# Down product of the last stage: all 1024 output columns at once in two passes over Strassen products, instead of two halves of 512 columns

## The chip, the cores and the metric

The kernel runs on one core of one Trainium2 chip. The metric is the device time of one execution in microseconds; where several runs are given, their median.

## The reference

The reference is one encoder layer on 512 tokens of width 1024 in float32. The part that changes is the last matrix product and the norm behind it:

```
h2 = rmsnorm(x1, g_pre_ffn)                       # x1: (512, 1024)
hid = depthwise_conv3(h2 @ w_up) + conv_b         # (512, 5632)
a, b = split(hid, 2)
y = x1 + rmsnorm((gelu(a) * b) @ w_down, g_post_ffn)   # w_down: (2816, 1024)
```

## The kernel before, in words

Every float32 matrix is held as a high part (rounded to the 32-bit format that TensorE multiplies at full pace) and a low part, and every product is three matmuls: high by high, high by low, low by high. A weight is prepared in one chain. SyncE loads a block of 128 rows by 1024 columns (512 KB) from `wall` into one of four `raw` buffers. ScalarE copies it to its high part (L100), VectorE subtracts that to get the low part (L119, function `split`). The parts lie in nine `w4` slots. `w_get` hands out the next unit of the list `units`, and prepares as many units ahead as slots allow; which instruction stands where on each engine is then set by a scheduler that orders the whole program ahead of time, each engine executing its own list in order.

The down product multiplies the gated hidden values `gp` (2816 features, 512 tokens) by `w_down`. Of its 22 blocks of 128 features, 18 are taken as nine couples (`DP`, index j), on which one level of Strassen's scheme (the Winograd form) runs: the two feature blocks of a couple, two halves of the tokens and two halves of the columns are its 2x2 matrices. That makes 7 products M1 to M7 in place of 8. The token side of the sums (A11, S1 to S4 and so on, function `down_forms`, names `fh`, `fl`, `fa`) is computed earlier on VectorE. The last four blocks (`WHOLE`) are multiplied without Strassen (`add_whole`, L1388).

Before, the columns are done in two halves of 512, each half a full sweep over the nine couples. A couple has two weight units. A "q" unit holds the three plain quarters (768 columns, loaded from memory), a "t" unit four sums (1024 columns) that VectorE forms by an add on 512 columns (L226) and two on 256 (L230, L231). Each of the 7 products fills one PSUM bank with two tiles of 128 tokens by 256 columns, so a couple is 42 matmuls with 256 columns (L1372). The eighth bank (M8) takes whole blocks. Behind the first half VectorE combines the banks into c11 to c22 (L1401 to L1417); behind the second, `token` adds the whole blocks, combines, scales (L1470 to L1488) and `rows` multiplies by the norm, adds x1 (L1520) and writes out. The norm's power is one GpSimd instruction on one column (L1488, `qr`). In the names of the profile, `dh` and `dl` are the high and low parts of a down unit, `wh` and `wl` those of a whole block, `cv` are convolution steps of the stage ahead, whose last part runs beside the start of the down product.

## Time and profile before

| | us |
|---|---|
| median of 3 runs (783.43 to 784.63) | 783.65 |
| span of the profiled execution | 782.6 |
| the down product: its first matmul starts, its last matmul starts | 668.8, 775.4 |
| busy TensorE / VectorE / ScalarE / GpSimd | 774.5 / 639.5 / 485.2 / 103.5 |

The span is that of one execution under the profiler, and all rows of the trace belong to it. In rows of instructions, the first number is the start and the second the duration, in microseconds; since an engine overlaps the end of one instruction with the next, the distance between starts is what an instruction costs. An "x" gives a count. A row of waits gives the microseconds waited in total, how often, and the longest.

### The profile page before, as it was taken

The page shows a single profiled execution, that of the slowest core. Times are in us where ns is not written, and L with a number is a line of the kernel's source. Part 1 is how long each engine was busy: PE and PEld are TensorE (multiplying, and loading weights), DVE is VectorE, ACT ScalarE, POOL GpSimd, SP SyncE. Part 2 cuts the span into 40 slices and gives each one's busy share as a digit, 9 for nine tenths or more (in the row PEclk, how much of TensorE's full clock was granted, in tenths as well). Part 3 has the DMA queues.
Part 4 walks back from the last instruction along what each step waited for, and adds up shares of the span by engine and source line. Part 5 has one row for each costly group of instructions (what it writes and reads, how often), then busy time and mean ns, then how long its engine had stood idle before and what let it go on. Part 6 is the DMA issues. An engine that isn't in the chain of part 4 may idle for free.

```text
span 782.6 us, 13472 instructions
## 1 busy us (share of the span) xinstructions
PE 774.5 (99%) x5139; PEld 720.7 (92%) x5139; DVE 639.5 (82%) x1093; ACT 485.2 (62%) x878; POOL 103.5 (13%) x132
## 2 busy tenths in 40 slices
PE   9999999999999999999999999999999999999996
PEld 8888998998999999999998998999999998999996
DVE  6567987789789988877765679989999889886987
ACT  7555568688466766644454686657777568644542
POOL 0040001130021102033211200001111012200001
PEclk9999999999999999999999999999999999999998
DMA  8783224453223233233459120435555375733344
GB/s 288 271 246 102 81 82 162 108 122 108 81 91 126 82 122 121 83 110 106 138 171 337 54 81 28 124 107 141 142 148 149 108 199 111 171 114 107 109 162 162
DMA packets 35889, 104.80 MB, mean 134 GB/s; under 512 B 4400, under 2 KB 6320, under 8 KB 35824
## 3 DMA queue, kind: packets, MB, share of 16 engines
q1 hardware_dynamic: 27936, 87.81, 34.0%
q0 software_dynamic: 7024, 14.95, 9.0%
q10 hardware_dynamic: 864, 1.18, 0.4%
q8 instruction: 40, 0.66, 0.4%
q14 instruction: 25, 0.20, 0.1%
HBM read 91.34 MB, written 4.19 MB: 122 GB/s over the span
## 4 chain that ended last, share of the span: by engine, by line
PE 92%; DVE 3%; DMA 3%; issue 1%; ACT 0%; POOLq 0%; DVEq 0%; POOL 0%; ACTq 0%
PE ps L926 24%; PE ps L300 12%; PE ps L302 12%; PE ps L301 12%; PE ps L1372 7%; PE ps L755 5%; PE ps L634 4%; PE ps L636 4%; PE ps L635 4%; DMA raw<-wall 3%; PE ps L1109 2%; PE ps L1108 2%; PE ps L1107 2%; DVE dl L119 1%; PE ps L997 1%
## 5 line engine op out<-in xcount | busy, mean ns | idle before, releaser
L119 DVE TENSOR_TENSOR wl<-raw,wh 128x1024 fp32r<-128x1024 f32 (+1 forms) x84 | 96.0, 1152 | 54.3 <-issue 19.1
L100 ACT ACTIVATE wf<-raw 128x512 fp32r<-128x512 f32 x140 | 85.6, 625 | 67.3 <-PE ps L301 19.4
L926 PE MATMUL ps<-sh,wf 128*128 128x256 f32 x640 | 117.4, 276 | 0.1
L119 DVE TENSOR_TENSOR wf<-raw,wf 128x512 fp32r<-128x512 f32 x140 | 107.0, 774 | 9.2 <-ACT wf L100 8.6
L926 PEld LDWEIGHTS ps<-sh,wf 128*128 128x128 f32 x640 | 101.9, 192 | 1.1 <-ACT sig L100 0.5
L100 ACT ACTIVATE wh<-raw 128x1024 fp32r<-128x1024 f32 (+2 forms) x88 | 84.8, 977 | 28.5 <-DMA raw<-wall 14.0
L300 PE MATMUL ps<-h2h,wh 128*128 128x512 f32 (+1 forms) x256 | 90.6, 354 | 0.0
L301 PE MATMUL ps<-h2l,wh 128*128 128x512 f32 (+1 forms) x256 | 90.4, 353 | 0.0
L302 PE MATMUL ps<-h2h,wl 128*128 128x512 f32 (+1 forms) x256 | 90.4, 353 | 0.0
L926 PE MATMUL ps<-sl,wf 128*128 128x256 f32 x320 | 88.0, 275 | 0.0
L926 PEld LDWEIGHTS ps<-sl,wf 128*128 128x128 f32 x320 | 61.4, 192 | 0.4
L1372 PE MATMUL ps<-dh,fh 128*128 128x256 f32 x216 | 59.6, 276 | 0.3 <-DVE yy L1409 0.3
L1372 PE MATMUL ps<-dl,fh 128*128 128x256 f32 x216 | 59.5, 275 | 0.0
L1372 PE MATMUL ps<-dh,fl 128*128 128x256 f32 x216 | 59.4, 275 | 0.0
L100 ACT ACTIVATE dh<-raw 128x768 fp32r<-128x768 f32 (+1 forms) x36 | 33.6, 950 | 33.8 <-DVE raw L231 15.2
L302 PEld LDWEIGHTS ps<-h2h,wl 128*128 128x128 f32 x256 | 48.6, 190 | 5.1
L301 PEld LDWEIGHTS ps<-h2l,wh 128*128 128x128 f32 x256 | 48.6, 190 | 4.5
L300 PEld LDWEIGHTS ps<-h2h,wh 128*128 128x128 f32 x256 | 48.6, 190 | 4.5
L926 PE MATMUL ps<-xh,wf 128*128 128x256 f32 x288 | 52.2, 275 | 0.0
L636 PE MATMUL ps<-wh,xl 128*128 128x512 f32 x128 | 48.5, 379 | 0.0
L635 PE MATMUL ps<-wl,xh 128*128 128x512 f32 x128 | 48.5, 379 | 0.0
L634 PE MATMUL ps<-wh,xh 128*128 128x512 f32 x128 | 48.5, 380 | 0.0
(343 smaller groups left out, 2171.6 us busy)
## 6 DMA issues: line engine op xcount, KB each, us to landing
raw<-wall SPq DMA_DIRECT2D x144, 512.0 KB, 3.7
x<-x SPq DMA_DIRECT2D x24, 256.0 KB, 6.0
fl<-gp POOLq DMA_DIRECT2D x12, 256.0 KB, 3.8
swap<-qkraw POOLq DMA_DIRECT2D x16, 128.0 KB, 4.8
x<-x POOLq DMA_DIRECT2D x8, 256.0 KB, 2.3
fl<-fs POOLq DMA_DIRECT2D x8, 256.0 KB, 4.3
xT<-xT SPq DMA_DIRECT2D x7, 256.0 KB, 5.0
xT<-xT POOLq DMA_DIRECT2D x4, 256.0 KB, 4.1
```

The source lines that it names most:

```text
L100: return nc.scalar.activation(out=o, in_=i, func=AF.Copy)
L119: low[0] = nc.vector.tensor_sub(lo, src, as32(hi)).ins
L300: nc.tensor.matmul(o, ah, bh, start=start, stop=False, skip_group_check=skip)
L301: nc.tensor.matmul(o, ah, bl, start=False, stop=False, skip_group_check=skip)
L302: pe_last[0] = nc.tensor.matmul(o, al, bh, start=False, stop=stop, skip_group_check=skip).ins
L634: nc.tensor.matmul(acc[t], xh[k][:, c], turns(wh[:, f]), start=k == 0, stop=False)
L635: nc.tensor.matmul(acc[t], xh[k][:, c], turns(wl[:, f]), start=False, stop=False)
L636: part_end[0] = nc.tensor.matmul(acc[t], xl[k][:, c], turns(wh[:, f]), start=False, stop=k == KD - 1)
L755: nc.tensor.matmul(bank[t], a_[:, c], turns(w_[:, f]), start=first and k == i == 0, stop=last and k == 3 and i == 2, skip_group_check=True,)
L926: self.last = nc.tensor.matmul(o, w_[:, c], a_, start=first and k == n == 0, stop=k == 3 and n == 2, skip_group_check=True,)
L1107: nc.tensor.matmul(o, ah, turns(bh), start=k == 0, stop=False)
L1372: nc.tensor.matmul(o, a_[:, c], turns(w_[:, f]), start=j == t == i == 0, stop=j == DP - 1 and i == 2 and n not in (M2, M3, M4), skip_group ...
```

## The change

All 1024 columns are done at once, so the two halves of the columns in Strassen's scheme are now the two halves of 512 of the whole width, and each product fills two PSUM banks (one tile of 128 tokens by 512 columns each). Eight banks hold four products, so the nine couples are swept twice. Pass 1 makes M1, M6, M5 and M4 (weights: the units "da" and "db", two products from each), pass 2 makes M2, M3 and M7 (units "dc" and "dd"). Matmuls have 512 columns, 24 per couple in pass 1 and 18 in pass 2; the last token tile's last part is still done in two halves of 256.

Each unit "da", "db", "dc" is one load of 512 KB, "dd" one of 256 KB. In "da" VectorE adds the loaded halves (L234); in "db" VectorE adds one piece (L236) and GpSimd another (L237), then `split` (now L121) follows; in "dd" VectorE adds one piece (L225). All whole blocks are used in pass 2's end, and two of them also in pass 1, after the couples 3 and 5 (`FILL`), so these two are loaded twice. The combination of the banks is L1408 (M6), L1412 (M5) and L1416 (M4) between the passes and L1468, L1470, L1478, L1484, L1488, L1497 at the end; the last step of the norm is L1447, its power L1440.

The core of the diff:

```diff
-            for _ in range(2):
-                pairs = [[("q", i + j), ("t", i + j)] for j in range(DP)]
-                whole = [[("blk", i + DP)], [("blk", i + DP + 1)]]
-                for u in pairs[:4] + whole[:1] + pairs[4:6] + whole[1:] + pairs[6:] if i == DOWN0 else pairs + whole:
-                    units += u
-                i += DP + WHOLE // 2
+            for j in range(DP):
+                units += [("da", j), ("db", j)] + ([("blk", WHOLE0 + FILL.index(j))] if j in FILL else [])
+            for j in range(DP):
+                units += [("dc", j), ("dd", j)]
+            units += [("blk", WHOLE0 + n) for n in range(WHOLE)]
+            i = NW
...
-    def w_down(form, i):
-
-        if form == "q":
-            raw = w_raw["q"] = raw_tile()
-            nc.sync.dma_start(raw, wall[i])
-            raw = raw[:, : 3 * 256]
+    def w_down(form, j):
+
+        i = DOWN0 + 2 * j
+        if form == "dd":
+            raw = raw_tile()[:, :S]
+            nc.sync.dma_start(raw, wall[i, :, S:])
+            nc.vector.tensor_add(raw, raw, w_raw["b"][:, S:])
+            w = slot("dt", 0, 1088)
+            lo, hi = w[:, AT_64 : AT_64 + S], w[:, S + AT_192 : 2 * S + AT_192]
         else:
-            b, raw = w_raw["q"], raw_tile()
-            two = "p (n c) -> p n c"
-            nc.vector.tensor_tensor(
-                out=raw[:, :512].rearrange(two, n=2), in0=b[:, :512].rearrange(two, n=2),
-                in1=b[:, None, 768:].to_broadcast([P, 2, 256]), op=ALU.add,
-            )
-            nc.vector.tensor_add(raw[:, 512:768], raw[:, :256], b[:, 256:512])
-            nc.vector.tensor_add(raw[:, 768:], raw[:, 512:768], b[:, 512:768])
-        w = 768 if form == "q" else 1024
-        at = 0 if form == "q" and (i - DOWN0) % (DP + WHOLE // 2) < 2 else AT_192
-        hi, lo = slot("dh", at, w), slot("dl", at, w)
+            raw = raw_tile()
+            nc.sync.dma_start(raw, wall[i + (form != "da")])
+            b1, b2 = raw[:, :S], raw[:, S:]
+            if form == "da":
+                w_raw["a"] = b2
+                nc.vector.tensor_add(b2, b1, b2)
+            elif form == "db":
+                nc.vector.tensor_add(b2, w_raw["a"], b2)
+                nc.gpsimd.tensor_tensor(out=b1, in0=b2, in1=b1, op=ALU.add)
+            else:
+                w_raw["b"] = raw
+            hi, lo = slot("dh", AT_192), slot("dl", AT_192)
...
+    def two_banks():
+        return [ps(), ps()]
+
+    def product(bank, w, at, act, j, first=0, last=DP - 1):
+
+        ah, al = dforms[j][act]
+        f = slice(at * S, (at + 1) * S)
+        for t in range(2):
+            c = slice(t * P, (t + 1) * P)
+            for i, (a_, n) in enumerate(((ah, 0), (ah, 1), (al, 0))):
+                nc.tensor.matmul(
+                    bank[t], a_[:, c], turns(w[n][:, f]), start=j == first and i == 0, stop=j == last and i == 2,
+                    skip_group_check=True,
+                )
...
+    m1, m6, m5, m4 = (two_banks() for _ in range(4))
     late = list(range(EAGER, DP))
-    c11, c12, c21, c22 = c4 = hi192("c", F32), lo64("c", F32), blk(n="c"), blk(n="c")
-    e1, e3, uu, yy = tmp("e1"), tmp("e3"), tmp("uu"), tmp("yy")
-
-    def after6():
-        v.tensor_add(uu, m[M6], e1)
-        v.tensor_sub(c12, m[M5], uu)
-        v.tensor_add(c12, c12, e3)
-
-    freed = []
-
-    def after7():
-        v.tensor_add(e1, m[M7], uu)
-        freed.append(v.tensor_sub(yy, m[M5], e1).ins)
-        v.tensor_add(c22, c22, yy)
-
-    steps = {
-        M1: lambda: copy(e1, m[M1]),
-        M2: lambda: v.tensor_add(c11, m[M2], e1),
-        M3: lambda: copy(e3, m[M3]),
-        M6: after6, M7: after7,
-        M4: lambda: v.tensor_add(c21, m[M4], e1),
-    }
+    ee = [hi192("c", F32), lo64("c", F32)]
+    pq, qq, uu = halves("c"), halves("c"), [tmp("uu") for _ in range(2)]
     for j in range(DP):
+        end = j == DP - 1
         if j < WHOLE:
             whole.append(two_parts(gp[2 * DP + j]))
         if j == 4:
             down_forms(late.pop(0))
-        products(m, j, *((steps, LOOK - 1) if j == DP - 1 else ()))
-        if j in (3, 5):
+        wa = w_get()
+        product(m1, wa, 0, "A11", j)
+        if end:
+            for t in range(2):
+                copy(ee[t], m1[t])
+        wb = w_get()
+        product(m6, wb, 1, "S2", j)
+        if end:
+            for t in range(2):
+                v.tensor_add(uu[t], m6[t], ee[t])
+        product(m5, wa, 1, "S1", j)
+        if end:
+            for t in range(2):
+                v.tensor_sub(pq[t], m5[t], uu[t])
+        product(m4, wb, 0, "A22", j)
+        if end:
+            for t in range(2):
+                v.tensor_add(qq[t], m4[t], uu[t])
+        if j in FILL:
             w = w_get()
-            for t in range(NT):
-                add_whole(m, t, [j // 2 - 1], [w], j == 5)
-            if j == 5:
-                copy(c22, m[M8])
+            for t in range(2):
+                add_whole(m4[t], 2 + t, [FILL.index(j)], [w])
...
+    m2, m3, m7 = (two_banks() for _ in range(3))
+    yy = halves("e")
     for j in range(DP):
+        wc = w_get()
+        if j < DP - 1:
+            product(m2, wc, 0, "A12", j, last=None)
+            product(m3, wc, 1, "S4", j, last=None)
+            product(m7, w_get(), 0, "S3", j)
         if j == 0:
             gpf.extend((hi192("gpf", F32), lo64("gpf", F32)))
             for i in range(2):
                 nc.gpsimd.dma_start(gpf[i], gffn[None, i * S : (i + 1) * S].to_broadcast([P, S]))
+    for t in (2, 0, 1, 3):
+        xt[t] = halves("x1")
+        for n in range(2):
+            nc.sync.dma_start(xt[t][n], x1[t][n])
+    product(m7, w_get(), 0, "S3", j)
+    for t in range(2):
+        v.tensor_add(qq[t], m7[t], qq[t])
+        square(2 + t, 0, qq[t])
+        v.tensor_sub(yy[t], pq[t], m7[t])
+    product(m2, wc, 0, "A12", j, last=None)
+    product(m3, wc, 1, "S4", j, last=None)
+    m8 = two_banks()
+    ww = [w_get() for _ in range(WHOLE)]
+    for t in range(2):
+        weighted(2 + t, 0, qq[t])
+    add_whole(m8[0], 2, (0, 1), ww[2:], None, True, True)
+    v.tensor_add(yy[0], m8[0], yy[0])
+    square(2, 1, yy[0])
+    weighted(2, 1, yy[0])
+    waiting = 2, scale(2, qn[2][:, 0:1], qn[2][:, 1:2])
+    for t in range(2):
+        add_whole(m2[t], t, (0, 1), ww[:2], None, False, True)
+        v.tensor_add(ee[t], m2[t], ee[t])
+        square(t, 0, ee[t])
+        weighted(t, 0, ee[t])
+        add_whole(m3[t], t, (0, 1), ww[2:], None, False, True)
+        v.tensor_add(pq[t], m3[t], pq[t])
+        square(t, 1, pq[t])
+        rows(*waiting)
+        waiting = t, scale(t, qn[t][:, 0:1], qn[t][:, 1:2])
+        weighted(t, 1, pq[t])
+    t = NT - 1
+    parts_ = (T0, slice(0, P)), (T1, slice(P, 256))
+    for n, (f, half) in enumerate(parts_):
+        add_whole(m8[1][:, f], t, (0, 1), ww[2:], half, n == 0, n == 1)
+        v.tensor_add(yy[1][:, f], m8[1][:, f], yy[1][:, f])
+        square(t, 1 + n, yy[1][:, f])
+        if n == 0:
+            v.scalar_tensor_tensor(
+                out=qn[t][:, 3:4], in0=qn[t][:, 0:1], scalar=EPS, in1=qn[t][:, 1:2], op0=ALU.add, op1=ALU.add
+            )
+            rows(*waiting)
+            weighted(t, 1, yy[1], f)
+    sc = scale(t, qn[t][:, 3:4], qn[t][:, 2:3], 0.0)
+    weighted(t, 1, yy[1], T1)
+    rows(t, sc, ((0, 512), (512, 768), (768, 1024)))
```

Order on VectorE around the fourth and fifth couple of pass 1 (numbers behind a name are buffers' numbers; `raw_7575` and `raw_7588` are the fourth couple's "da" and "db", 7618 the first whole block, 7630 and 7659 the fifth couple). Before, in the first half of the columns, at the fourth couple:

```order
L119 TENSOR_TENSOR dl_7619<-raw_7614,dh_7618 128x1024
L226 TENSOR_TENSOR raw_7708<-raw_7674 128x512
L119 TENSOR_TENSOR wl_7653<-raw_7650,wh_7652 128x1024
L230 TENSOR_TENSOR raw_7708<-raw_7708,raw_7674 128x256
L1291 TENSOR_TENSOR gp_7054<-gp_7054 128x256
L231 TENSOR_TENSOR raw_7708<-raw_7708,raw_7674 128x256
L1292 TENSOR_TENSOR gp_7054<-gp_7065,fs_7823 128x256
L119 TENSOR_TENSOR fl_7829<-fs_7823,fh_7828 128x512
L119 TENSOR_TENSOR dl_7677<-raw_7674,dh_7676 128x768
```

After:

```order
L121 TENSOR_TENSOR dl_7579<-raw_7575,dh_7578 128x1024
L121 TENSOR_TENSOR dl_7593<-raw_7588,dh_7592 128x1024
L234 TENSOR_TENSOR raw_7630<-raw_7630 128x512
L1297 TENSOR_TENSOR gp_7054<-gp_7054 128x256
L121 TENSOR_TENSOR fl_7727<-fs_7721,fh_7726 128x512
L1298 TENSOR_TENSOR gp_7054<-gp_7065,fs_7721 128x256
L121 TENSOR_TENSOR fl_7731<-gp_7065,fh_7730 128x512
L236 TENSOR_TENSOR raw_7659<-raw_7630,raw_7659 128x512
L121 TENSOR_TENSOR wl_7621<-raw_7618,wh_7620 128x1024
L234 TENSOR_TENSOR raw_7673<-raw_7673 128x512
L121 TENSOR_TENSOR dl_7634<-raw_7630,dh_7633 128x1024
L121 TENSOR_TENSOR fl_7735<-gp_7054,fh_7734 128x512
```

The three adds that form a "t" unit are gone; each unit now has one 512-column add ahead of a 1024-column subtract, two such units per couple, and an add stands up to six places ahead of the subtract of its own unit.

Order on GpSimd around the end of the convolution; the DMAs form the low parts of activations. Before:

```order
L1273 DMA fl_7398<-fs_7392 128x512
L1273 DMA fl_7403<-gp_6622 128x512
L1273 DMA fl_7408<-gp_6611 128x512
L1273 DMA fl_7496<-fs_7490 128x512
L1273 DMA fl_7501<-gp_6855 128x512
L1273 DMA fl_7506<-gp_6844 128x512
L1540 DMA gpf_8248<-gffn 128x512
```

After:

```order
L1279 DMA fl_7399<-fs_7393 128x512
L237 TENSOR_TENSOR raw_7445<-raw_7445 128x512
L1279 DMA fl_7404<-gp_6622 128x512
L1279 DMA fl_7409<-gp_6611 128x512
L237 TENSOR_TENSOR raw_7545<-raw_7545 128x512
L1279 DMA fl_7498<-fs_7492 128x512
L1279 DMA fl_7503<-gp_6855 128x512
L1279 DMA fl_7508<-gp_6844 128x512
L237 TENSOR_TENSOR raw_7588<-raw_7588 128x512
```

GpSimd has an add of 128x512 per couple of pass 1 between those DMAs and behind them.

Order on VectorE at the change of passes: 7834 and 7847 are the last couple of pass 1, 7873 with 7885, 7909 with 7915 and 7929 with 7971 the first three couples of pass 2 ("dc" with "dd"). Before, at the change of column halves (L1414 to L1417 combine the banks):

```order
L119 TENSOR_TENSOR dl_8092<-raw_8087,dh_8091 128x1024
L1414 TENSOR_TENSOR c_7511<-ps_7536,e_1282_7515 128x512
L119 TENSOR_TENSOR dl_8143<-raw_8140,dh_8142 128x768
L1401 TENSOR_TENSOR uu_7517<-ps_7565,e_1282_7515 128x512
L1402 TENSOR_TENSOR c_7512<-ps_7558,uu_7517 128x512
L1408 TENSOR_TENSOR e_1282_7515<-ps_7572,uu_7517 128x512
L1403 TENSOR_TENSOR c_7512<-c_7512,e_1283_7516 128x512
L1409 TENSOR_TENSOR yy_7518<-ps_7558,e_1282_7515 128x512
L119 TENSOR_TENSOR dl_8190<-raw_8185,dh_8189 128x1024
L1410 TENSOR_TENSOR c_7514<-c_7514,yy_7518 128x512
```

After:

```order
L225 TENSOR_TENSOR raw_7885<-raw_7885,raw_7873 128x512
L121 TENSOR_TENSOR dl_7838<-raw_7834,dh_7837 128x1024
L121 TENSOR_TENSOR dl_7852<-raw_7847,dh_7851 128x1024
L121 TENSOR_TENSOR dl_7876<-raw_7873,dh_7875 128x1024
L121 TENSOR_TENSOR dt_7888<-raw_7885,dt_7888 128x512
L225 TENSOR_TENSOR raw_7915<-raw_7915,raw_7909 128x512
L121 TENSOR_TENSOR dl_7912<-raw_7909,dh_7911 128x1024
L1408 TENSOR_TENSOR uu_7526<-ps_7514,c_7520 128x512
L1408 TENSOR_TENSOR uu_7527<-ps_7515,c_7521 128x512
L1412 TENSOR_TENSOR c_7522<-ps_7516,uu_7526 128x512
L225 TENSOR_TENSOR raw_7971<-raw_7971,raw_7929 128x512
L121 TENSOR_TENSOR dt_7918<-raw_7915,dt_7918 128x512
```

The adds that read the banks M6 and M5 (L1408, L1412) now stand behind the second L225, and the third L225 between them; before, a subtract or two stood there and no add on a loaded block.

Order on VectorE at the very end. Before:

```order
L1470 TENSOR_TENSOR z_8895<-ps_8772,e_8184 128x256
L1480 SCALAR_TENSOR_TENSOR q_8180<-q_8180 128x1
L1520 SCALAR_TENSOR_TENSOR zg_8436<-zg_8436,qr_8850,x_1463_8820 128x512
L1487 TENSOR_TENSOR qs_8898<-q_8180 128x1
L1520 SCALAR_TENSOR_TENSOR zs_8849<-zs_8849,qr_8850,x_1464_8821 128x512
L1477 TENSOR_TENSOR zs_8896<-z_8895,gpf_8249 128x256
L1520 SCALAR_TENSOR_TENSOR zg_8564<-zg_8564,qr_8897,x_1471_8867 128x512
L1520 SCALAR_TENSOR_TENSOR zs_8896<-zs_8896,qr_8897,x_1472_8868 128x256 x2
```

After:

```order
L1435 TENSOR_TENSOR zs_8394<-e_7970,gpf_8002 128x256
L1447 SCALAR_TENSOR_TENSOR zs_8347<-zs_8347,qr_8368,x_1429_8223 128x512
L1500 SCALAR_TENSOR_TENSOR q_7962<-q_7962 128x1
L1447 SCALAR_TENSOR_TENSOR zs_8372<-zs_8372,qr_8368,x_1430_8224 128x512
L1497 TENSOR_TENSOR e_7970<-ps_8264,e_7970 128x256
L1435 TENSOR_TENSOR zs_8394<-e_7970,gpf_8002 128x256
L1439 SCALAR_TENSOR_TENSOR qs_8412<-q_7962 128x1
L1447 SCALAR_TENSOR_TENSOR zs_8267<-zs_8267,qr_8411,x_1431_8227 128x512
L1447 SCALAR_TENSOR_TENSOR zs_8394<-zs_8394,qr_8411,x_1432_8228 128x256 x2
```

Of the two last-but-one steps of the third written tile (L1520 before, L1447 after, each 128x512), both stood behind the last add from PSUM (L1470); now they stand ahead of it (L1497).

167 lines of the change are left out of this document (35 added, 132 removed).

## Prediction

> **What bounds the kernel now.** I read the page's totals first, then the chain of waits, then the waits of TensorE in the last stage.
>
> ```profile
> span 782.6 us, 13472 instructions
> PE 774.5 (99%) x5139; PEld 720.7 (92%) x5139; DVE 639.5 (82%) x1093; ACT 485.2 (62%) x878; POOL 103.5 (13%) x132
> PE 92%; DVE 3%; DMA 3%; issue 1%; ACT 0%; POOLq 0%; DVEq 0%; POOL 0%; ACTq 0%
> 668.92 15.98 PE ps L1372 x143
> PE ps L1372 <- DVE yy L1409: 0.3, 1, 0.3
> ```
>
> TensorE is busy for 99% of the span and is 92% of the chain. In the stage that changes it waits once, 0.3 us, at the change of column halves. So the stage is worth what its matmuls take, as long as the weight work of VectorE stays ahead; whatever makes a weight late is added in full. The profiled execution spans 782.6 us, 1.05 below the median of 783.65; I add that 1.05 at the end.
>
> **Matmuls: 4.4 us less.** The timeline of TensorE gives the two paces and the ends of the stage (the first row of each pair is 16 matmuls ahead of the second).
>
> ```profile
> 662.50 0.38 PE L301 MATMUL ps<-h2l,wh 128*128 128x512 f32 x1
> ...
> 665.95 0.38 PE L302 MATMUL ps<-h2h,wl 128*128 128x512 f32 x1
> ...
> 668.76 0.27 PE L1372 MATMUL ps<-dh,fa 128*128 128x256 f32 x1
> ...
> 775.37 0.28 PE L1388 MATMUL ps<-wh,fl 128*128 128x256 f32 x1
> ```
>
> Sixteen matmuls with 512 columns take 3.45 us, 215.6 ns each; the chain row above gives 15.98/143 = 111.7 ns with 256 columns. Before, the stage has 756 + 192 = 948 matmuls of 256 columns; after, 378 + 84 = 462 of 512 and 24 of 256, the same columns in all. First start to last start is 775.37 - 668.76 = 106.61 us now, and would be 462 x 0.2156 + 24 x 0.1117 - 0.11 = 102.2 with no wait: 4.4 less, of which 0.8 is idle time that before has (106.61 - 947 x 0.1117). The Trainium skill's TensorE: Matmul & The Clock Gate ("Wait — 56ns, not 53.3ns?") puts the interval at columns/2.4 + 2.5 ns, which is 215.8 ns for 512, as here, but 109.2 for 256 where the row has 111.7; by the page the matmuls would fall by only 1.2 us instead of 3.5. The row decides.
>
> **VectorE in pass 1: 3.8 us of waits.** The windows are ten us of the stage each (columns: window, length, PE, PEld, DVE, ACT, POOL with counts, clock, DMA share, GB/s); the rows behind them are the last weight of the fourth couple.
>
> ```profile
> 669.00:679.00 10.00, 10.00 (x92) 10.00 (x91) 8.41 (x13) 9.56 (x16) 2.59 (x3) 1.00 0.69 160
> 679.00:689.00 10.00, 10.00 (x90) 9.87 (x90) 9.91 (x19) 4.92 (x7) 1.12 (x2) 1.00 0.58 182
> ...
> 699.00:709.00 10.00, 10.00 (x92) 10.00 (x91) 5.99 (x10) 2.98 (x5) 0.00 (x0) 1.00 0.34 107
> ...
> 683.77 1.22 DVE L119 TENSOR_TENSOR dl<-raw,dh 128x1024 fp32r<-128x1024 f32 x1
> ...
> 684.84 0.28 PE L1372 MATMUL ps<-dh,fh 128*128 128x256 f32 x1
> 685.05 0.38 PE L1372 MATMUL ps<-dl,fh 128*128 128x256 f32 x1
> ```
>
> VectorE is nearly full until 689, because the convolution and the splits of activations still run, and free afterwards. The subtract that ends at 684.99 is used by the matmul at 685.05, which comes 0.1 us late: there is no slack at this place already. The price list, from the timeline (the start of the next row is the pitch):
>
> ```profile
> 656.59 0.95 DVE L119 TENSOR_TENSOR dl<-raw,dh 128x768 fp32r<-128x768 f32 x1
> ...
> 660.04 0.69 DVE L226 TENSOR_TENSOR raw<-raw 128x512 f32<-128x512 f32 x1
> 660.64 0.42 DVE L1291 TENSOR_TENSOR gp<-gp 128x256 f32<-128x256 f32 x1
> ...
> 661.65 1.22 DVE L119 TENSOR_TENSOR dl<-raw,dh 128x1024 fp32r<-128x1024 f32 x1
> 662.78 0.42 DVE L231 TENSOR_TENSOR raw<-raw,raw 128x256 f32<-128x256 f32 x1
> 663.12 0.75 DVE L1250 SCALAR_TENSOR_TENSOR cv<-ps,part,cv 128x511 f32<-128x511 f32 x1
> ...
> 311.23 1.77 POOL L208 TENSOR_TENSOR raw<-raw,raw 128x512 f32<-128x512 f32 x1 [8.62 <-DMA raw<-wall]
> ...
> 311.77 1.77 DVE L119 TENSOR_TENSOR wf<-raw,wf 128x512 fp32r<-128x512 f32 x1
> ...
> 313.80 0.68 DVE L119 TENSOR_TENSOR wf<-raw,wf 128x512 fp32r<-128x512 f32 x1
> ...
> DVE cv L1250 <- ACT cv L1247: 1.5, 1, 1.5
> ```
>
> A subtract of 1024 columns costs 1.14 us, an operation on 512 costs 0.60, on 256 0.34 to 0.42 (I take 0.36), a convolution step 0.67. The change gives GpSimd an add of 128x512 per couple of pass 1 (L237), where before it has none here. The nearest row is L208 in an earlier stage: beside it a VectorE subtract with two SBUF inputs takes 1.77 instead of 0.68 us, 1.09 more. Such a hold costs 0 where VectorE waits anyway and 1.09 where it has an operation ready. I count 0.75, 0.6, 1.0 and 1.05 for the four adds up to the fourth couple (it is full there; the first two I take to fall partly into gaps of VectorE) and 1.05 for the next. The Trainium skill's SBUF — State Buffer ("Who interferes with whom") calls this an exclusive lock that one side holds for its whole instruction; that row agrees in kind (the subtract ended 0.5 us after the add), and by the rule a subtract that comes just behind the start of an add would lose the add's whole length, up to 1.77 in that row, 0.7 more.
>
> The first weight's subtract stands where it stood, at 656.59. From it to the second unit's subtract of the fourth couple, the order has 8 subtracts of 1024, 13 operations of 512, 12 of 256 and 8 convolution steps: 9.1 + 7.8 + 4.3 + 5.4 = 26.6 us. With holds of 3.4 and a wait for ScalarE of 1.1 (1.5 in the row, less 0.4 of the holds ahead of it) it is ready at 687.7. TensorE wants it after three couples of 24 matmuls, six of M1 and one of M6: 668.76 + 3 x 5.17 + 1.5 = 685.8. Then come 3 subtracts, 7 of 512 and 2 of 256, 8.3 us, a hold of 1.05 and 0.2 of waiting: the fifth couple's second unit is ready at 697.3 and wanted, after the first whole block (12 matmuls, 2.59), at 668.76 + 4 x 5.17 + 2.59 + 1.5 = 693.5. So TensorE has lost 3.8 us by there. Without holds the same sum gives 0.8, and with all at 1.09 and the ScalarE wait in full, 4.6: the bounds. Behind it VectorE needs 3.5 + 1.05 = 4.5 us per couple against 5.17 of TensorE, so it catches up and no more is lost until the end of the pass.
>
> **Loads and the change of passes: 0.3 + 1.8 us.**
>
> ```profile
> raw<-wall SPq DMA_DIRECT2D x21, 512.0 KB, 3.5
> DVE raw L226 <- DMA raw<-wall: 10.2, 6, 2.5
> ```
>
> A load lands 3.5 us after its issue. In pass 1 a couple brings 1 MB per 5.17 us instead of 0.5 MB per 4.69; two loads in 5.17 us is inside what the first windows moved. Before, the first add waits up to 2.5 us for a load, at no cost, since nothing urgent is behind it. After, SyncE can issue the half load of a "dd" unit only when a raw buffer is free (four buffers), and VectorE's add for it (L225) stands in its order ahead of other work. The first one stands ahead of the last couple's two subtracts: its load is issued after the subtract before, so they come 0.3 us late (0 to 1). The second stands ahead of the adds that empty the banks of M6 and M5: the last subtract of the pass, 1.74 us of splits, then the load at 3.5, add 0.60, subtract 1.14, two adds 1.2: the banks of M6 are empty 6.4 us after that subtract. TensorE wants them 4 x 1.29 = 5.2 us after it first uses that weight. VectorE's third and fourth adds to empty M5 have two other operations between them and lose about 1 us more. From this 2.3 I take off 0.5, as the subtract will be that much ahead of its use: 1.8, between 0 (VectorE 2.3 us ahead) and 3. Before had 0.3 there. Pass 2 needs 2.34 us of VectorE per 3.88 us and 0.75 MB; nothing is late there. The blocks loaded a second time come by SyncE alone and lie beside M7 and M2; the last lands just in time, 0.
>
> **Tail: 1.4 us.**
>
> ```profile
> 775.69 0.42 DVE L1470 TENSOR_TENSOR z<-ps,e 128x256 f32<-128x256 f32 x1
> ...
> 776.09 0.75 DVE L1520 SCALAR_TENSOR_TENSOR zg<-zg,qr,x 128x512 f32<-128x512 f32 x1
> ...
> 777.05 0.93 POOL L1488 TENSOR_TENSOR qr<-qs,nhalf 128x1 f32<-128x1 f32 x1 [1.66 <-DVE qs L1487]
> ...
> 778.68 0.87 DVE L1520 SCALAR_TENSOR_TENSOR zs<-zs,qr,x 128x256 f32<-128x256 f32 x2
> ...
> 779.58 0.33 SPq L1523 DMA_DIRECT2D out<-zs  x1
> ```
>
> Now the last add from PSUM starts 0.32 us after the last matmul's start, the power on GpSimd at 1.68, and VectorE ends at 779.55, 4.2 after. In the new order the two 0.67 us steps of the tile before stand ahead of that add, and they wait for that tile's own power: its last bank ends 24 matmuls of which half are narrow (2.7 us) before the end, and add, square on ScalarE and power (0.4 + 0.7 + 1.1, as in these rows, with 0.7 more for a 512 add) take it to 0.5 after the last start. So: steps until 1.9, add until 2.3, square and sum until 3.1, power until 4.1, then 0.67 + 2 x 0.34 to 5.55: 1.4 more. Low 0.8, if the power comes earlier; high 2.0, if the output transfer that ScalarE issues just ahead of the last square holds it.
>
> **Sum.** -4.4 + 3.8 + 0.3 + 1.8 + 1.4 = +2.9: span 785.5, median 786.5.
>
> **The rivals.** (a) The holds fall where VectorE waits, and it comes to the pass change ahead: -4.4 + 0.8 + 0.3 + 1.4 = -1.9, 781.7 us, faster. For it: 1.6 us of VectorE is idle in 669 to 679. Against: the row at 685.05 is late before any hold. It decides from below 1.4 us of waits in both passes together. (b) About half of the waits come: -4.4 + 1.9 + 0.2 + 0.9 + 1.4 = 0, 783.7. For it: half of my holds are guessed from their neighbours. (c) The doubled loads of pass 1 land a us later each, with two under way; the waits at the third and fourth couples grow by 2.2 in all: 788.7. Against: the window with 182 GB/s has no late load on TensorE's path. That the 512-column pace is not had is no rival: L301 and L302 show it with weights moving.
>
> **How the numbers follow.** My forecast has 0.5, (a) 0.2, (b) 0.2, (c) 0.1. Below and above 0.2% (1.57 us, about what a measurement can tell from no change) are: faster 0.22 (a, and a little of b), same 0.2, slower 0.58. The forecast's own range is 784.8 to 788.2; the range that leaves out half of (a) and part of (c) is 781.7 to 788.8.
>
> **What would show it.** Right: 512-column matmuls 215.6 ns apart; subtracts of 1024 that take about 2.2 instead of 1.22 us beside L237; waits of TensorE for VectorE at the weights of the fourth and fifth couples, together near 4; VectorE waiting for the load at its second L225, then TensorE for the adds from M6 and M5; VectorE's end 5.5 us after the last matmul's start. Wrong: subtracts at 1.22 beside GpSimd's adds, no idle TensorE in pass 1 or at the change of passes, or a pace other than 215.6.

## The result and the profile after

The changed kernel takes 792.1 us (median of 5 runs, 789.63 to 794.38) against 783.65 (783.43 to 784.88): 8.5 us more, a ratio of 1.0107 with a 95% interval of 1.0089 to 1.0126. The forecast was slower, at 786.5 and at most 788.8. The profiled execution is the one of 794.38 us, the slowest of the five, with a span of 792.6, 10.0 above the span of before; what the trace accounts for is thus about 2 us more than the median shows.

The page's totals and the chain of waits:

```profile
span 792.6 us, 12553 instructions
PE 774.9 (98%) x4677; PEld 706.0 (89%) x4677; DVE 639.3 (81%) x1051; ACT 485.8 (61%) x864; POOL 119.3 (15%) x141
PE 85%; DVE 6%; DMA 5%; issue 2%; ACT 1%; POOL 0%; DVEq 0%; POOLq 0%; SPq 0%; ACTq 0%
```

TensorE is still 98% busy by the page, but its share of the chain fell from 92 to 85%. The waits of TensorE in the last stage, of which before had one of 0.3 us:

```profile
PE ps L1372 <- DVE cv L1260: 6.4, 2, 4.4
PE ps L1384 <- DVE wl L121: 2.2, 1, 2.2
PE ps L1384 <- DVE e L1497: 0.5, 1, 0.5
```

Not one of the three is what the prediction named. The largest is for `cv`, a step of the convolution, not for a weight. TensorE's timeline at that place (start, duration, and in brackets the idle time and what ended it):

```profile
672.60 0.38 PE L1372 MATMUL ps<-dh,fl 128*128 128x512 f32 x1
674.98 0.45 PE L1372 MATMUL ps<-dh,fh 128*128 128x512 f32 x1 [2.00 <-DVE cv L1260]
675.27 0.38 PE L1372 MATMUL ps<-dl,fh 128*128 128x512 f32 x1
675.48 0.38 PE L1372 MATMUL ps<-dh,fl 128*128 128x512 f32 x1
680.30 0.77 PE L1372 MATMUL ps<-dh,fh 128*128 128x512 f32 x1 [4.44 <-DVE cv L1260]
680.86 0.63 PE L1372 MATMUL ps<-dl,fh 128*128 128x512 f32 x1
681.28 0.63 PE L1372 MATMUL ps<-dh,fl 128*128 128x512 f32 x1
```

The 18 matmuls of M1, M6 and M5 of the first couple run at the full pace. The three of M4's first tile come 2.2 us late, those of its second tile 4.6 us. (Lateness is counted here from the start that the pace would give; the rows of waits give idle time, which is up to 0.2 less.) Nothing is wrong with their weights, which are the other half of the unit that M6 has used already. These are the first matmuls into M4's two PSUM banks, the last two of eight, and those still held the last two results of the up product, until the convolution had read them. Behind the wait, matmuls start 0.42 us apart instead of 0.216. The windows give the reason in the third number from the end (the granted clock; the columns are those of the prediction's windows):

```profile
669.00:679.00 10.00, 4.86 (x22) 3.63 (x20) 8.63 (x13) 7.17 (x12) 4.94 (x5) 0.90 0.71 149
679.00:689.00 10.00, 8.70 (x32) 7.39 (x33) 9.96 (x14) 6.57 (x10) 1.60 (x1) 0.76 0.66 189
689.00:699.00 10.00, 10.00 (x48) 8.76 (x47) 9.88 (x13) 4.61 (x6) 2.70 (x2) 1.00 0.59 185
...
769.00:779.00 10.00, 10.00 (x41) 8.41 (x40) 6.00 (x12) 2.17 (x6) 1.11 (x2) 0.83 0.14 52
```

The clock was half for 6.8 us, from 676.97 within the wait for the second tile to 683.79, and for 3.4 us from 769.12, after the wait of 2.2 us for a whole block's low part that ends at 768.5. Before, it is 1.00 throughout the stage.

Laid side by side with the ideal, where a matmul with 512 columns takes 0.2157 us and one with 256 takes 0.1117: from first to last start the stage is 784.89 - 668.93 = 115.96 us long. Of this, 462 x 0.2157 + 23 x 0.1117 = 102.22 is that pace and 13.74 is lost: 6.84 for M4's banks, 1.80 for the half clock behind them, 0.14 at the change of passes, 2.33 for the whole block and 1.79 for the half clock behind it, 0.68 at the last tile, and 0.16 in small pieces. So the matmuls did save 106.61 - 102.22 = 4.4 us, and with 0.2 of later start and 0.5 behind the last matmul the sum is -4.4 + 13.7 + 0.7 = 10.0, the difference of the spans.

Why the banks were late shows on VectorE, GpSimd and ScalarE:

```profile
650.10 1.66 DVE L1256 SCALAR_TENSOR_TENSOR cv<-c,part,cv 128x511 f32<-128x511 f32 x1
...
665.54 1.12 DVE L1298 TENSOR_TENSOR gp<-gp,fs 128x256 f32<-128x256 f32 x1
...
670.30 2.14 POOL L237 TENSOR_TENSOR raw<-raw 128x512 f32<-128x512 f32 x1 [1.10 <-DVE raw L236]
...
671.21 1.51 DVE L1295 TENSOR_TENSOR fs<-gp,gp 128x256 f32<-128x256 f32 x1
672.75 0.42 DVE L1296 TENSOR_TENSOR fs<-fs,gp 128x256 f32<-128x256 f32 x1
...
673.27 0.63 ACT L102 ACTIVATE fh<-fs 128x512 fp32r<-128x512 f32 x1 [2.73 <-DVE fs L1296]
...
674.09 0.74 DVE L1260 SCALAR_TENSOR_TENSOR cv<-ps,part,cv 128x511 f32<-128x511 f32 x1
...
677.35 0.76 ACT L1253 ACTIVATE cv<-ps,part 128x512 f32<-128x512 f32 x1
...
678.14 0.75 DVE L1256 SCALAR_TENSOR_TENSOR cv<-ps,part,cv 128x511 f32<-128x511 f32 x1 [1.25 <-ACT cv L1253]
...
679.41 0.74 DVE L1260 SCALAR_TENSOR_TENSOR cv<-ps,part,cv 128x511 f32<-128x511 f32 x1
```

The holds that the prediction counted are there: L1295 takes 1.51 instead of 0.42 us beside GpSimd's third add, and beside the first two adds L1256 takes 1.66 instead of 0.74 and L1298 takes 1.12 instead of 0.42. Together that is 2.7 of the 4.1 us by which L1296 comes later than its like before (672.75 against 668.63 for L1290); the rest is not taken apart here. But what suffers is not the weight behind a hold. ScalarE waits for L1296, does seven operations, and only then starts the last convolution (L1253), and the last L1260 frees the bank at 680.15. In before the same two steps ran here:

```profile
674.02 0.75 DVE L1250 SCALAR_TENSOR_TENSOR cv<-ps,part,cv 128x511 f32<-128x511 f32 x1 [1.49 <-ACT cv L1247]
...
675.29 0.74 DVE L1254 SCALAR_TENSOR_TENSOR cv<-ps,part,cv 128x511 f32<-128x511 f32 x1
```

They ended at 676.0, and nobody waited: the first half of the columns began with seven products of one bank each, and the eighth bank (M8) was first used by the whole block behind the fourth couple. With four products of two banks each, the eighth bank is wanted 21 matmuls, 4.5 us, after the pass begins, at about 673.5. So even at the time of before it would have been 2.6 us late.

### The profile page after: what moved, and what is told of

It is laid out like the page before. It is cut to its first block, busy times and chain, and to the rows that moved or that the text cites. A ratio compares the mean times of both kernels' runs of the same rounds, so it can differ in the third digit from the quotient of the medians.

```text
span 792.6 us, 12553 instructions
## 1 busy us (share of the span) xinstructions
PE 774.9 (98%) x4677; PEld 706.0 (89%) x4677; DVE 639.3 (81%) x1051; ACT 485.8 (61%) x864; POOL 119.3 (15%) x141
## 4 chain that ended last, share of the span: by engine, by line
PE 85%; DVE 6%; DMA 5%; issue 2%; ACT 1%; POOL 0%; DVEq 0%; POOLq 0%; SPq 0%; ACTq 0%
PE ps L932 23%; PE ps L306 11%; PE ps L308 11%; PE ps L307 11%; PE ps L761 5%; DMA raw<-wall 4%; PE ps L1372 4%; PE ps L640 3%; PE ps L642 3%; PE ps L641 3%; PE ps L1384 2%; PE ps L1114 2%; PE ps L1113 2%; PE ps L1115 2%; DVE dl L121 2%
## 5 line engine op out<-in xcount | busy, mean ns | idle before, releaser
L121 DVE TENSOR_TENSOR wl<-raw,wh 128x1024 fp32r<-128x1024 f32 (+1 forms) x86 | 99.0, 1160 | 55.2 <-ACT wh L102 22.2
L121 DVE TENSOR_TENSOR wf<-raw,wf 128x512 fp32r<-128x512 f32 x140 | 105.8, 765 | 10.0 <-ACT wf L102 9.0
L102 ACT ACTIVATE wh<-raw 128x1024 fp32r<-128x1024 f32 (+2 forms) x90 | 87.0, 980 | 30.7 <-DMA raw<-wall 15.6
L932 PEld LDWEIGHTS ps<-xh,wf 128*128 128x128 f32 x288 | 45.6, 192 | 0.2
L102 ACT ACTIVATE dh<-raw 128x1024 fp32r<-128x1024 f32 x27 | 28.3, 1053 | 27.0 <-POOL raw L237 14.1
L1372 PE MATMUL ps<-dh,fh 128*128 128x512 f32 x90 | 34.6, 384 | 6.4 <-DVE cv L1260 6.4
L932 PE MATMUL ps<-xl,wf 128*128 128x256 f32 x144 | 39.6, 275 | 0.0
```

Source lines behind the costliest of these rows:

```text
L102: return nc.scalar.activation(out=o, in_=i, func=AF.Copy)
L121: low[0] = nc.vector.tensor_sub(lo, src, as32(hi)).ins
L932: self.last = nc.tensor.matmul(o, w_[:, c], a_, start=first and k == n == 0, stop=k == 3 and n == 2, skip_group_check=True,)
L1372: nc.tensor.matmul(bank[t], a_[:, c], turns(w[n][:, f]), start=j == first and i == 0, stop=j == last and i == 2, skip_group_check=True,)
```

## The experiments

Theory A: M4's banks are the loss. Theory B: GpSimd's holds alone. Theory C, the prediction's: weights that VectorE prepares late. In the tables of waits below, the columns are the total, the count and the longest, in us. The runs come from four sessions, in which the median of before lay between 783.17 and 783.77 us; the ratios are to the before of the same session. The scheduler orders the whole program anew for each edit, so an edit can also move work that it does not name.

**The add L237 on VectorE.**

```diff
-                nc.gpsimd.tensor_tensor(out=b1, in0=b2, in1=b1, op=ALU.add)
+                nc.vector.tensor_tensor(out=b1, in0=b2, in1=b1, op=ALU.add)
```

> The change with one edit: the add L237 runs on VectorE instead of GpSimd. Theory A (the wait of TensorE in pass 1 is for M4's two PSUM banks, which the last convolution steps on VectorE free; GpSimd's adds only push these steps back): operations of VectorE beside L237 no longer take 1.1 to 1.5 us instead of 0.4, the last L1260 ends 1 to 2 us earlier, TensorE's waits there go from 6.8 to 4 to 6 us, total 789 to 791. Theory B (GpSimd's holds are the loss itself): the waits go below 2 us and the total to 783 to 786. If neither hold nor place of this add matters: 791 to 793.

787.35 us (786.15 to 788.27), ratio 1.0053 (1.0036 to 1.007). Its waits:

```profile
PE ps L1372 <- DVE cv L1260: 3.5, 1, 3.5
PE ps L1384 <- DVE e L1497: 0.5, 1, 0.5
```

The first tile's bank is now on time, the second 3.6 us late, with one half clock of 3.4 us behind it (1.76 us lost). The whole block's low part is on time too. So moving this one add is worth 4.2 us (by the ratios, 1.0107 to 1.0053), more than Theory A expected and less than Theory B did, and the wait for the bank stays without it: A, made worse by B. How much of the 4.2 the holds are is not settled. Between the two traces, 3.2 us of the difference lie at M4's banks and their half clock, where the holds act, but 4.0 lie at the whole blocks near the end, long after GpSimd's last add of the pass, where here the third block's copy had no load to wait for.

**The first couple's M4 behind the second couple's M5.**

```diff
+        if j == 0:
+            wb0 = wb
+            continue
+        if j == 1:
+            product(m4, wb0, 0, "A22", 0)
         product(m4, wb, 0, "A22", j)
```

> The change with one edit: the first couple's M4 is done after the second couple's M5, so that M4's banks are first wanted about 3.9 us later; the same matmuls in another order. Theory A (banks): the waits of 2.2 and 4.6 us shrink to 3 us or less in one place, TensorE's clock stays full there, and the total falls by 5 to 7 us, to 785 to 787. Theory C (the prediction's: weights late at the fourth and fifth couples): TensorE waits for low parts of the third to fifth couples instead, 3 to 6 us, and the total falls by less than 2, 790 to 793.

793.41 us (792.13 to 795.19), ratio 1.013 (1.0113 to 1.0146), no better. The bank wait is gone, and this came in its place:

```profile
PE ps L1372 <- DVE dl L121: 4.9, 2, 2.9
PE ps L1384 <- DVE wl L121: 1.0, 1, 1.0
PE ps L1372 <- DVE c L1412: 0.8, 1, 0.8
PE ps L1372 <- DVE uu L1408: 0.8, 1, 0.8
PE ps L1384 <- DVE e L1502: 0.5, 1, 0.5
```

These are waits of the prediction's kind: low parts (`dl`) in two places, 5.2 us by the starts, but at the second and third couple (677.06 and 687.41) and not at the fourth and fifth, then the banks of M6 and M5 at the change of passes, 2.1 us. Each of the two waits for weights also brought a half clock of 3.4 us, 1.7 us lost each. The first, 3.1 us, was there all along: the second couple's low part is ready at 677.0 here and was ready at 676.9 in the changed kernel, where the bank wait hid it. The second, 2.1 us, is this edit's own: the third couple's low part is ready at 687.4 here and was ready at 683.7 there. (The edit holds the first couple's weight slots 3.9 us longer, and in VectorE's order that subtract now stands behind splits of activations.)

**TensorE kept busy in the waits**, by 10 and 20 matmuls with a weight of zeros:

```diff
+            idle(10)    # matmul(m1[0][:16], zero, turns(wb[0][:, :S]), start=False, stop=False)
+            product(m4[:1], wb, 0, "A22", j, tiles=(0,))
+            idle(20)
+            product(m4, wb, 0, "A22", j, tiles=(1,))
```

> The change as it is, and TensorE kept busy in its two waits of the first couple: 10 and 20 matmuls of 512 columns by a weight of zeros, added to a bank of M1 (they add nothing), ahead of the first and the second tile of M4. Theory (the halved clock behind the wait is caused by the idle time, not by the work that follows): the clock stays full in 670 to 690, and the total falls by about 1.8 us, to 789.5 to 791. Rival (the clock falls for another reason, such as the kind of matmul): it falls there all the same, and the total stays at 791.5 to 793.

796.62 us (794.92 to 797.63), ratio 1.0159 (1.0146 to 1.0172). The windows:

```profile
669.00:679.00 10.00, 10.00 (x47) 6.15 (x46) 8.38 (x12) 7.18 (x13) 5.16 (x5) 1.00 0.72 152
679.00:689.00 10.00, 9.05 (x41) 6.83 (x39) 9.90 (x17) 5.79 (x10) 1.68 (x2) 1.00 0.54 144
689.00:699.00 10.00, 8.21 (x30) 6.94 (x31) 6.52 (x7) 3.48 (x4) 1.17 (x1) 0.83 0.50 158
```

The clock stayed full where the zeros filled the waits, with the same matmuls behind them, so it takes idle time to halve it. The total lies above both ranges: TensorE waited 2.8 us at 690.79 for the third couple's second low part, and a half clock followed. That part was ready only at 690.7, against 683.7 in the changed kernel, since its subtract now stood behind splits and sums of activations in VectorE's order; so the total tells nothing of what the full clock is worth.

**M2's first whole blocks ahead of M8's.**

```diff
+    add_whole(m2[0], 0, (0, 1), ww[:2], None, False, True)
     add_whole(m8[0], 2, (0, 1), ww[2:], None, True, True)
```

> The change with one edit: behind the last couple, the whole blocks of M2's first tile (12 matmuls on blocks 0 and 1) are done ahead of M8's first tile (blocks 2 and 3). Theory: the fourth block's low part is late because its slot is freed by the last couple's M2 and M3; 12 matmuls ahead of it cover the wait of 2.2 us, the clock stays full there (1.7 us more), the total falls by about 4, to 787 to 789. Rival (that block's load is late by itself): the wait stays and moves, 791 to 793.

790.74 us (790.68 to 792.26), ratio 1.0099 (1.0084 to 1.0114). The wait of 2.2 us for `wl` and the half clock behind it are gone (0.19 us lost there), as expected, but the wait at the last tile's bank grew from 0.68 to 1.54, and the total fell by less than half of 4 us. That the slot made the block late, as the expectation says, is not what the trace of the changed kernel shows: its copy was done at 764.4, and VectorE's subtract came late.

**All of these together**, and a bank of its own for the last 256 columns; and that bank alone with L237 on VectorE:

```diff
+    m9 = ps()
-        add_whole(m8[1][:, f], t, (0, 1), ww[2:], half, n == 0, n == 1)
+        o = (m8[1], m9)[n][:, :256]
+        add_whole(o, t, (0, 1), ww[2:], half, True, True)
```

> The three edits together (L237 on VectorE, the first couple's M4 after the second's M5, M2's first tile ahead of M8's), and a bank of its own for the last tile's last 256 columns, so that the last matmuls do not wait 0.7 us for VectorE's read. If the waits and the slow clock found in the profile are the whole loss: TensorE waits under 2 us in the stage, clock full, 780 to 782.5. If weights are the next limit in pass 1: a wait of 1 to 4 us for low parts of the third to fifth couples, 783 to 786.

> The change with L237 on VectorE and a bank of its own for the last 256 columns of the last tile. Theory: the last matmuls wait 0.7 us because they write a bank that VectorE is reading; with a bank of their own this wait is gone and the total is 0.5 to 0.8 below the run with L237 on VectorE alone (787.4), 786.6 to 786.9. Rival: the end is set by VectorE's chain, not by these matmuls, and the total stays, 787.2 to 787.6.

Together: 789.23 us (786.17 to 790.15), ratio 1.0068 (1.0046 to 1.0089), no better than L237 on VectorE alone. The clock is 1.00 to the end of the stage, but waits of 0.4 to 1.4 us for weights and at the change of passes sum to 5.8 us, and VectorE ends 6.2 us after the last matmul's start instead of 4.4. The bank alone: 788.72 us (788.19 to 789.89), ratio 1.0071 (1.0057 to 1.0085). The 0.7 us wait is gone and VectorE ends 5.2 instead of 4.4 us after the last matmul's start. The end is set by VectorE's chain, as the rival said. The total is above both ranges; its profiled execution began the stage 1.6 us later than that of L237 on VectorE alone (669.99 against 668.39), as its clock was half until 9.1 us of the span instead of 4.3.

**Half of M4 moved**, with L237 on VectorE and the bank (the second tile, behind the second couple's M6), and the same without the bank but with VectorE's work that is needed later (four splits of activations, the last couple's sums, the two whole blocks) moved back by two or three couples. The late work was also tried without the rest, with L237 on VectorE and on GpSimd:

```diff
+        if j == 1:
+            product(m4, wb0, 0, "A22", 0, tiles=(1,))
...
-FILL = (3, 5)
+FILL = (5, 7)
-        if j < WHOLE:
+        if 3 <= j < 3 + WHOLE:
```

> As the one with L237 on VectorE and the bank of its own, and the second tile of the first couple's M4 (three matmuls) is done behind the second couple's M6, 12 matmuls or 2.6 us later. Banks theory: the wait of 3.6 us falls to about 1, short enough that the clock stays full, and 1.8 us of slow clock go too: 782.5 to 784. Weights theory: what is won there is lost again in waits for low parts of the third to sixth couples: 785 to 787.

> The change with L237 on VectorE, and with work of VectorE that is not yet needed moved out of the start of pass 1: the splits of the four whole blocks' activations stand at the couples 3 to 6 instead of 0 to 3, the last couple's activation sums at couple 6 instead of 4, and the two whole blocks of pass 1 at the couples 5 and 7 instead of 3 and 5. Theory: the wait for M4's second bank (3.6 us, and 1.8 of half clock) stays, since the convolution steps stand in the same place, and the total stays near that of the run with L237 on VectorE alone, 786 to 788. Rival: with less work ahead of them, the last convolution steps come earlier too, the wait falls below 2 us and the total to 783 to 785.

> The same moves, but with L237 on GpSimd as in the change. Theory (holds push the convolution steps back): the waits of 2.2 and 4.6 us and the half clock stay, 789 to 792. If VectorE's load of splits was the cause of the late banks: the waits fall below 4 us together and the total to 784 to 787.

> L237 on VectorE, the late work as in g2, and the second tile of the first couple's M4 behind the second couple's M6. If banks and VectorE's load at the start are together the whole loss of pass 1: no wait over 1 us in pass 1, full clock, 781.5 to 784, near or below before. If the loop of four raw buffers is the next limit: waits of 1 to 2 us for low parts at the sixth to eighth couples remain, 784 to 787.

In this order: 790.57 us (788.12 to 792.81), 788.97 (787.59 to 789.16), 792.05 (791.45 to 792.25) and 789.7 (787.25 to 793.88). Moving the late work leaves the bank waits as they are (3.7 us with VectorE, 2.2 and 4.1 with GpSimd), so they do not come from that work. With half of M4 moved the bank wait is 0.9 us and the clock full, and waits of 1 to 1.7 us come up at weights, at the change of passes and in one run at a whole block instead. No version that computes the whole product had a median under 787.

**The passes in the other order**, M2, M3, M7 and the whole blocks first, then the rest, L237 on VectorE or on GpSimd (the loops and the end are rewritten to match; the order of the units shows it):

```diff
             for j in range(DP):
-                units += [("da", j), ("db", j)] + ([("blk", WHOLE0 + FILL.index(j))] if j in FILL else [])
+                units += [("dc", j), ("dd", j)] + ([("blk", WHOLE0 + FILLS[j])] if j in FILLS else [])
             for j in range(DP):
-                units += [("dc", j), ("dd", j)]
-            units += [("blk", WHOLE0 + n) for n in range(WHOLE)]
+                units += [("da", j), ("db", j)]
+            units += [("blk", WHOLE0 + n) for n in range(2)]
```

> The same products with the passes in the other order: M2, M3 and M7 first (units dc and dd, 2.3 us of VectorE per 3.9 us of TensorE, six banks), with M8 and the whole blocks of M2, M3 and M8 in this pass, then M1, M6, M5, M4 (L237 on VectorE), the last two couples' M4 and two whole blocks at the end. Theory: both limits at the start go (banks still held by the convolution, VectorE too full for the units da and db), TensorE waits under 2 us in the stage at full clock, and the end grows by 1 to 2 us, since more sums stand there: 779 to 782.5, faster than before. Rival: the copies out of the banks at the change of passes or the sums at the end take back what is won, 783 to 788.

> The same with L237 on GpSimd again, now in the second pass, where VectorE has no convolution left. If a hold only costs where VectorE is full: within 1 us of the run with L237 on VectorE. If it costs everywhere: 2 us more or over.

803.26 us (801.37 to 804.9) and 802.74 (802.15 to 803.41). The start did get better: in the first 15 us of the stage 1.7 us are lost, against 8.6 in the changed kernel. But the copies out of the banks cost 3.5 us at the change of passes and the end is far worse:

```profile
PE ps L1384 <- DVE c L1516: 8.9, 1, 8.9
PE ps L1372 <- ACT c L102: 3.3, 1, 3.3
PE ps L1372 <- DVE dt L121: 1.6, 2, 0.8
PE ps L1372 <- DVE e L1411: 1.6, 2, 1.4
```

The last tile's second half waits 8.9 us, because VectorE's read of the first half stands behind all the sums of the end. As a faster version it failed. The two totals agree within their scatter, so in a pass where VectorE is not full, GpSimd's add costs nothing that shows in the total.

**The weight sums of pass 1 left out** (L234, L236, L237; so a part of the product is not computed as it should be), as it is and with the first couple's M4 behind the second's M5:

```diff
-                nc.vector.tensor_add(b2, b1, b2)
...
-                nc.vector.tensor_add(b2, w_raw["a"], b2)
-                nc.gpsimd.tensor_tensor(out=b1, in0=b2, in1=b1, op=ALU.add)
+                pass
```

> The change without the weight sums of pass 1: L234, L236 and L237 are left out (the units da and db are split as loaded), so VectorE has 1.2 us less per couple and GpSimd no add. If the banks alone make a wait: TensorE still waits 2 to 4 us for M4's second bank and runs 1.8 us at half clock, nothing else in pass 1, and the total is 785 to 788. If the bank wait is only an effect of the sums: no wait over 1 us in pass 1, 779 to 782.

> The same with the sums left out, and the first couple's M4 behind the second couple's M5. If banks and VectorE's weight work are together the whole loss of pass 1: no wait over 1 us and full clock there, what is left is the change of passes (0 to 2), the last blocks and the end, 780 to 783. If a third limit is hidden behind them (loads, raw buffers): waits of 1 us or more for low parts or loads remain in pass 1, 784 to 787.

787.94 us (785.25 to 789.03) and 785.31 (783.45 to 786.64), ratios 1.0051 (1.0031 to 1.0071) and 1.0024 (1.0014 to 1.0034). The waits of the first:

```profile
PE ps L1370 <- DVE cv L1258: 3.7, 1, 3.7
PE ps L1382 <- DVE e L1495: 0.5, 1, 0.5
```

Without any sum the second bank is late by 3.8 us, as with the sums on VectorE (3.6), and nothing else in pass 1 is: the banks are a limit of their own, and neither this run nor the next has a wait for a load there. With M4 moved too, 2.5 us are still lost, and a half clock with them, at a low part of the third couple, which stands behind the rest of the activations' work in VectorE's order while the first couple's weight slots are held. So even without its sums the new pass does not get below the time of before.

## Why the prediction was wrong

**The matmuls** were right: 4.4 us were forecast, and at the pace measured, 215.7 ns a matmul, they come to 4.4.

**The step that failed** is the sentence that the stage is worth what its matmuls take as long as VectorE's weight work stays ahead, and that whatever makes a weight late is added. I asked of every weight when it is ready and of no bank when it is free. The plan names it: eight banks for four products, where before had one bank to spare until the fourth couple. The row of before that would have told it is VectorE's L1254 at 675.29, set against a first use at 673.5. None of the rivals had this wait.

**The half clock** had no term at all. It added 1.8 us behind each of the two long waits: 3.6 us of the 10.0.

**VectorE in pass 1**, 3.8 us forecast. The mechanism was right and hidden: the fourth couple's two low parts were ready at 690.0 (forecast 687.7). Without any wait TensorE would want the later one at 668.93 + 79 x 0.2157 = 686.0, but held up by the banks it came only at 694.6:

```profile
658.49 1.21 DVE L121 TENSOR_TENSOR dl<-raw,dh 128x1024 fp32r<-128x1024 f32 x1
...
687.63 2.36 DVE L121 TENSOR_TENSOR dl<-raw,dh 128x1024 fp32r<-128x1024 f32 x2
```

Most of the 2.3 us by which the forecast missed this time is in its starting point: the first weight's subtract did not stand where it stood, at 656.59, but at 658.49, with a new add (L236) and the first hold ahead of it. The bounds 0.8 and 4.6 do not come out of the prediction's own sum: without holds it gives no wait (fifth couple ready at 693.2, wanted at 693.5), with all in full 5.2; the middle of 3.8 does. Where the banks are out of the way, the waits for weights are 5.2 us (M4 moved) or, with TensorE kept busy, 2.8 in one place, both partly of those edits' making. The holds of GpSimd are about as forecast in size (0.9, 0.7 and 1.1 us for the first three, against 0.75, 0.6 and 1.0), but what they cost TensorE here goes through an activation's sum, ScalarE's order and the last convolution step, not through a subtract.

**The change of passes**, 0.3 + 1.8: 0.14 measured. VectorE did wait for the load at its second L225, 2.4 us, as named, but the adds from M6 were done at 730.2, and TensorE wanted its banks at 730.6. With M4 moved TensorE came there at the same time (730.4), but that load made VectorE wait 3.9 us, and 2.1 us were lost at the two adds that the prediction named. So the term was right in kind, and whether it costs 0 or 2 hung on when one load landed; that it was near 0 here is luck.

**The whole blocks** at the end were put at 0 (just in time): 2.3 us of wait, and 1.8 of half clock. This is the second step that failed. The fourth block's load and copy were done by 764.4, but its subtract stood behind five operations of VectorE's until 767.26, and these stood behind the third block's subtract, which waited for its copy, and that for its load. I had looked at the last load alone and not at VectorE's order behind the third:

```profile
762.04 1.06 ACT L102 ACTIVATE wh<-raw 128x1024 fp32r<-128x1024 f32 x1 [1.80 <-DMA raw<-wall]
...
763.12 1.23 DVE L121 TENSOR_TENSOR wl<-raw,wh 128x1024 fp32r<-128x1024 f32 x1 [1.63 <-ACT wh L102]
...
767.26 1.21 DVE L121 TENSOR_TENSOR wl<-raw,wh 128x1024 fp32r<-128x1024 f32 x1
```

With L237 on VectorE the order at this place is the same, the third subtract waits for no load, and TensorE loses under 0.2 us.

**The tail**, 1.4: VectorE ends 4.4 us after the last matmul's start (784.89) against 4.2, and that matmul is 0.7 late for VectorE's read: 0.9 in all, inside the bounds of 0.8 to 2.0. That is partly luck, as VectorE's chain, on which the term rests, gave only 0.2 of it. The last row:

```profile
787.73 1.54 DVE L1447 SCALAR_TENSOR_TENSOR zs<-zs,qr,x 128x512 f32<-128x512 f32 x3 [0.66 <-POOL qr L1440]
```

The sign came out right for another reason than the one forecast. Of the losses in the sum, the two largest terms hardly showed (3.8 was hidden, 2.1 was 0.1), and the bank wait, the whole block and the half clock, which had no term or were put at 0, came in their place with 6.8 + 2.3 + 3.6 = 12.7 us.

## What to carry to other kernels

A change that gives each product more PSUM banks moves forward the moment at which the last bank must be free: list the banks, who reads them last and when, beside the list of weights. Price any forecast wait of TensorE of about 2 us or more with the half clock that may follow it. Where two waits overlap, the one that the profile names hides the other, and taking it away shows only what comes next; leave out the suspected work altogether, as the weight sums here, to see each alone. And look in each trace whether the edit also moved other work, as it did with M4 moved and with TensorE kept busy, before its total is read as the price of one cause.

## What the runs showed of the hardware

The clock drops come in pieces of 3.41 us, and one costs 1.7 to 1.8 us of matmuls. (At the first place of the changed kernel two pieces follow each other; the first lies mostly in the wait, and both together cost 1.8.) A wait of 2.1 us was followed by one (687.41, M4 moved), waits of 1.4 to 1.7 were not, and neither was the one of 3.8 us at M4's second bank without the weight sums. The clock records of the traces say why. Within each of the 16 profiled executions, all changes of the clock lie whole multiples of 3.413 us apart: in the changed kernel 2, 25, 1 and 5 of them from the drop at 676.97 on. So time is cut into windows of 3.413 us, and the idle time of TensorE within one window can be read off (length less busy time; the granted clock is the third number from the end). First the two windows that hold the 3.8 us wait without the weight sums, then the window of the whole block's wait in the changed kernel and the one behind it:

```profile
671.81:675.23 3.42, 1.46 (x7) 0.94 (x5) 1.49 (x2) 3.39 (x7) 1.52 (x2) 1.00 0.97 270
675.23:678.64 3.41, 1.70 (x8) 1.54 (x9) 3.41 (x6) 3.41 (x6) 0.21 (x1) 1.00 0.92 174
...
765.71:769.12 3.41, 1.24 (x7) 0.76 (x6) 3.37 (x5) 0.72 (x2) 0.00 (x0) 1.00 0.00 0
769.12:772.54 3.42, 3.42 (x10) 2.67 (x9) 1.54 (x3) 0.72 (x2) 0.28 (x1) 0.50 0.00 0
```

The 3.8 us fell across the edge of two windows, 2.0 us in one and 1.7 in the other, and the clock stayed full; the 2.3 us lay in one window, 2.2 by this count, and the next window ran at half. Over all traces, from the first full clock on, each of the 29 windows at full clock with 2.1 us or more of idle time was followed by half clock, and none with under 1.9 us was; the two between went one each way (1.92 did, 1.95 did not). So what counts in these runs is the idle time within one window, not the length of the wait. The Trainium skill's TensorE: Matmul & The Clock Gate ("Part 1: The HAM clock gate") describes a free-running activity window of 3.4 us, and the traces agree with it. The same page's advice to avoid gaps over about 3 us ("Why this matters for your kernels") is too generous here, as a wait of 2.1 us within one window was enough.

How the windows lie against the program differs from one execution to the next: the first change to full clock comes anywhere from 3.4 to 9.1 us after the start of the span. That would also explain the spread between executions of one kernel. Without the weight sums, the profiled execution, with its wait and no half clock, took 785.25 us at a mean clock of 0.998, and the other three took 787.55 to 789.03 at 0.993 to 0.995. That these three lost their time by it is only argued, since no profile of them was kept; the changed kernel's wide spread (789.63 at 0.994, 794.38 at 0.992) fits.
